# One block of a macaron encoder: attention scores from [qh; qh] and [ql; 0] times [kh; kl], k of both heads transposed in one group, changed orders in the feed-forward and at its joint, last output block in halves

## The chip, the cores and the metric

The kernel runs on one core of one Trainium2 chip. The metric is the device time of one execution in microseconds (us). Before the change it is 1906.35 us, the median of three runs (1906.08 to 1906.64).

## What is computed

The input x has 1024 rows (frames) of 1024 columns, float32. One layer is computed, in three steps:

```python
x = x + 0.5 * swiglu(rms_norm(x, n1), w1_in, w1_out)        # D = 1024, F = 2816
x = x + stick_breaking_attention(rms_norm(x, nm), w_qkv, q_gain, k_gain, w_o)
x = x + 0.5 * swiglu(rms_norm(x, n2), w2_in, w2_out)
# attention, 16 heads of 64: q, k are rms-normed per head and have a gain
z = (q @ k.T) / 8                                           # s < t only
A[t, s] = sigmoid(z[t, s]) * prod(1 - sigmoid(z[t, j]) for s < j < t)
o = A @ v                                                   # then o @ w_o
```

## The kernel before, in words

**Split products.** TensorE multiplies operands of type fp32r. Every float32 operand is therefore split in a high part and the rest ("h" and "l", `split` L195: a copy on ScalarE, then a subtraction on VectorE or GpSimd), and a product is three matmuls: h·h, h·l and l·h (`mm3` L301).

**Feed-forward** (`ffn_in` L430, `ffn_out` L558, used twice). The products are done by a scheme with seven products of half-size blocks instead of eight. `ffn_in` goes over 11 slices q of the hidden columns; for each one `prepare` (L466) splits the weights and their mixtures s1, s2, s3, s4 into units ("u" tiles), and `seven` (L494) runs seven products of 12 matmuls for the gate and seven for the up half. Two of the banks go on accumulating after a copy: `copy` (L497) takes the bank "ka" to SBUF on ScalarE, and the next product into "ka" can start after it. ScalarE thus does the units' high parts (L196), the copies (L499) and the silu of the gates (L547). `ffn_out` runs seven products m in the order of `SEVEN`, each on four banks, one for each block of 128 rows. The last, m = 6, ends block by block: block t takes the last three of the six chunks (five slices, 15 matmuls of 512 columns), then `result(t)` (L619) adds the bank to x, then `at(...)` is called, which in the second feed-forward stores the rows to the output (L1349). The results of the product before it, m = 2, are done late, during the first chunks of the last one.

**Joint between the first feed-forward and the attention** (`at` L872). After block t of the last product, rows that are normed already are transposed into the banks "mb" (`turn_rows`, L287) and split, and the next rows are squared (ScalarE), their rates taken (GpSimd) and scaled (`norm` L251, VectorE). The numbers (2, 0, 0, 1) at L900 say how many row blocks are transposed after block 0, 1, 2, 3.

**Attention** (L912 to L1247). The heads are done in eight pairs p. For each pair `qkv` (L956) makes q, k and v of the next pair in 24 pieces ("fills"), on banks "bq"; q and k are kept in a tile qk, whose columns are six groups of 64: q of both heads, then k of head 1 twice, k of head 0 twice, scaled by the norm's factor on GpSimd (L996, L999). `prep_q` (L1023) transposes the q of both heads of half the frames with four transposes of 128x128 (L1016), and puts, for each head, the high part on one half of the partitions of a tile q_s (ScalarE, L1020) and the rest on the other half (VectorE, L1021). `prep_k` (L1031) does the same for one head and half the frames: the transposed k stands on both halves of the partitions; kh_s holds its high part, kl_s the rest. A score step (`scores` L1038) is then two matmuls with the same stationary operand (L1057, L1058):

```python
for i in range(2):
    pe.matmul(z[:, : off + n], q, state["k", hd, kb][i][:, keys], start=i == 0, stop=i == 1)
```

[qh; ql]·[kh; kh] gives qh·kh + ql·kh, and [qh; ql]·[kl; kl] gives the terms with kl. Two sigmoids follow on ScalarE (L1062), the running product on VectorE (L1067) and the weights on GpSimd (L1074). The weights are transposed (L1098), split and multiplied by v (L1119, `values` L1080). Sums of a pair are written to DRAM in two parts (L1132) and loaded again before the output projection (L1143).

**What sets the order.** Each pair has four parts a, b, c, d of 10, 14, 21 and 16 units of planned time (`PARTS` L39). In part a the scores of head 1, second half of the frames are made; in b head 0, first half; in c head 1, first half; in d those of head 0, second half of the next pair. `put(part, t, f)` gives a step a planned time; the steps are emitted in that order (L1246), and a scheduler of the framework then orders each engine's instructions by this priority as their operands come ready; `issue_after` adds an edge between two instructions. The preparations stand at: q of the second half at c 15.0, k of head 0 of the second half at c 17.0, k of head 1 of the second half at d 8.0, q of the first half at a 5.0, k of head 0 of the first half at a 7.5, k of head 1 of the first half at b 10.7 (L1216 to L1222). All large transfers, the raw weights of pair p+2 among them (c 14.0, c 15.0, d 9.0, d 10.0, L941), are issued in order from SP's queue.

Of the kernel before, what the change touches and what calls it, by code (L numbers as in the profile page):

```python
# [52 lines left out]
)  # L53

# [59 lines left out]
def macaron_kernel(ctx, tc, x, g1, w1_in, w1_out, gm, w_qkv, gq, gk, w_o, g2, w2_in, w2_out, out):  # L114
# [155 lines left out]
    def turned(xs, tb, bk, tl=None):  # L270
# [13 lines left out]
        for d in range(2):  # L284
# [5 lines left out]
            split(tp, xh[dst], xl[dst])  # L290
# [139 lines left out]
    def ffn_in(pl, w_in, keep, tl, hb, right, last):  # L430
# [35 lines left out]
        def prepare(raw, behind=None):  # L466
# [20 lines left out]
            marks["s3"] = marks["unit"]  # L487
# [6 lines left out]
        def seven(us, result):  # L494


            def copy(b):  # L497
                s = small(pl, "s")
                act.activation(s, b, AF.Copy)  # L499
                return s  # L500
# [13 lines left out]
            s2 = copy(a)  # L514
            product(c, us["s4"], b22, False)
# [11 lines left out]
        for q in range(1, NQ):  # L527
# [21 lines left out]
            us = prepare(stream(pl, w_in, q, 1), before[1, 1][:, 0:1] if q == 1 else None)  # L549
# [8 lines left out]
    def ffn_out(pl, w_out, keep, x_from, ahead, at):  # L558
# [37 lines left out]
        for m, tag, fresh, goes in SEVEN:  # L596
# [11 lines left out]
            def add(ts, cs):  # L608
                for c in cs:
                    (wh, wl), (hh, hl), _ = ops[c]  # L610
                    for i, q in enumerate(CHUNKS[c]):
                        for t in ts:
                            s = slice(t * P, (t + 1) * P)
                            mm3(
                                bs[t], [((hh[:, i, s], hl[:, i, s]), (wh[:, i], wl[:, i]))],
                                fresh and q == 0, q == NQ - 1, not fresh,
                            )

            def result(t, bs=bs, goes=goes):  # L619
                for (th, h), sign in goes:  # L620
                    xc = x_sb[h][:, 4 * (1 - th) + t, :]
                    dve.scalar_tensor_tensor(out=xc, in0=bs[t], scalar=0.5 * sign, in1=xc, op0=ALU.mult, op1=ALU.add)
# [43 lines left out]
    with pools(*RAWS) as pr:  # L666
# [200 lines left out]
        with banks("ps2"), pools(*SECOND) as pl:  # L867
# [4 lines left out]
            def at(x_sb, m, where, ops):  # L872
# [25 lines left out]
                elif m == 6 and str(where).startswith("block"):  # L898
                    t = int(where[-1])
                    turn_rows("mb", (2, 0, 0, 1)[t])  # L900
                    squares(pn, row, (t,), half[:, t : t + 1], (1,))
                    last_norm = lambda: pending.extend(norm(pn, row, (t,), gain_m, half[:, t : t + 1], pooled=True))
                    if t < 3:
                        last_norm()
                    else:
                        late.append(last_norm)
# [9 lines left out]
    with ExitStack() as stack:  # L916
# [39 lines left out]
        def qkv(p, state):  # L956


            def start(half):
                if half:  # L960
                    state["v"] = pl[f"vst{p % 2}"].tile([P, NT, 4, DH], F32R, name="vst", bufs=1)
                state["qk", half] = pl[f"qk{half}"].tile([P, 4, 6, DH], F32, name=f"qk{half}", bufs=1)
# [14 lines left out]
            def finish(half, i, ps, room):  # L977
# [16 lines left out]
                rk = r[:, :, 0:1].unsqueeze(3).to_broadcast([P, 4, 2, DH])  # L994
                kv = qk[:, :, 2:3, :].to_broadcast([P, 4, 2, DH])
# [23 lines left out]
        def parts(tp, g, hi, lo):  # L1019
            act.activation(hi, tp, AF.Copy, scale=g)  # L1020
            dve.scalar_tensor_tensor(out=lo, in0=tp, scalar=g, in1=hi.bitcast(F32), op0=ALU.mult, op1=ALU.subtract)  # L1021

        def prep_q(state, half):  # L1023

            tp = turned_qk(state["qk", half], 0)
            for i in range(2):
                own, other = slice(i * DH, (i + 1) * DH), slice((1 - i) * DH, (2 - i) * DH)
                q_s = state["q", i, half] = pl[f"st{half}"].tile([P, NHALF], F32R, name=f"q_s{half}")
                parts(tp[own], g_sb[0][own], q_s[own], q_s[other])

        def prep_k(state, hd, half):  # L1031

            kh_s, kl_s = state["k", hd, half] = [
                pl[f"st{half}"].tile([P, NHALF], F32R, name=f"k{n}_s{half}") for n in "hl"
            ]
            parts(turned_qk(state["qk", half], 4 - 2 * hd), g_sb[1], kh_s, kl_s)

        def scores(state, hd, half):  # L1038
# [3 lines left out]
            def step(tb, kb):  # L1042
# [7 lines left out]
                q = state["q", hd, half][:, (tb % 4) * P : (tb % 4 + 1) * P]  # L1050
# [6 lines left out]
                for i in range(2):  # L1057
                    pe.matmul(z[:, : off + n], q, state["k", hd, kb][i][:, keys], start=i == 0, stop=i == 1)  # L1058
# [21 lines left out]
        def values(state, p, hd, half):  # L1080

            own, other = slice(hd * DH, (hd + 1) * DH), slice((1 - hd) * DH, (2 - hd) * DH)
# [23 lines left out]
            def apply(sbs):  # L1106
# [19 lines left out]
                if hd == 1 and (p < NP - 2 or p == NP - 2 and half):  # L1126
# [3 lines left out]
                    split(o, oh, ol)  # L1130
# [28 lines left out]
        last_x = ((pool_e, 0, lambda: xl[:, KD - 1, T - P : T - P + 1].bitcast(F32)),)  # L1159
# [27 lines left out]
        for p in range(-1, NP):  # L1187
# [21 lines left out]
            if nxt is not None:  # L1209
# [6 lines left out]
                put("c", 15.0, partial(prep_q, nxt, 1))  # L1216
                put("c", 17.0 if p >= 0 else 20.0, partial(prep_k, nxt, 0, 1))
                put("d", 8.0, partial(prep_k, nxt, 1, 1))
            if this is not None:
                put("a", 5.0, partial(prep_q, this, 0))  # L1220
                put("a", 7.5, partial(prep_k, this, 0, 0))
                put("b", 10.7, partial(prep_k, this, 1, 0))  # L1222
            if 0 <= p < NP - 2:

                held = (
                    ((pool_e, 1, lambda s=nxt: s["qk", 1][:, 0, 4, 0:1]),),
# [165 lines left out]
```

## Time and profile before

| | before |
|---|---|
| median of 3 runs | 1906.35 us (1906.08 to 1906.64) |
| the profiled execution | 1906.09 us |
| its span, first to last instruction | 1904.3 us |
| TensorE (PE) busy | 1892.7 us, 99% |
| VectorE (DVE), ScalarE (ACT), GpSimd (POOL) busy | 1230.2, 975.7, 1138.2 us |
| granted clock of TensorE | 1.000 |
| attention, from the first q to the end of the projection | about 660 to 1290 us of the span |

Times in the views are microseconds from the start of the span. A line is named L and its number in the listing; where a helper does the work, the line is the helper's. Matmuls are pipelined: the duration of one is longer than the distance to the next, so what a matmul costs is read from the starts of neighbours. PE stands for matmuls, PEld for the loads of stationary operands, SPq for the queue that issues transfers. "Idle" behind a row is the time that the engine stood still before it, and what ended it.

### The profile page before, as it was taken

How to read it: one execution, taken by the hardware profiler on the slowest of the kernel's cores; microseconds unless marked ns; L12 is line 12 of the kernel's file. 1: busy time of each engine (PE TensorE's matmuls, PEld its weight loads, DVE VectorE, ACT ScalarE, POOL GpSimd, SP SyncE). 2: the span in 40 equal slices, each digit the busy share in tenths (PEclk: the TensorE clock that was granted, in tenths of full speed). 3: DMA queues.
4: the chain of work that ended last, by engine and by line, in shares of the span. 5: the costliest groups of instructions: out<-in, count | busy, mean ns of one | idle time of the engine just before them, and what ended most of it. 6: DMA issues, size and time to landing. Idle time of an engine off the chain costs nothing.

```text
span 1904.3 us, 26681 instructions
## 1 busy us (share of the span) xinstructions
PE 1892.7 (99%) x9330; PEld 1620.3 (85%) x9330; DVE 1230.2 (65%) x1713; ACT 975.7 (51%) x1794; POOL 1138.2 (60%) x1063
## 2 busy tenths in 40 slices
PE   9999999999999999999999999999999999999999
PEld 8878888888888799999999997788888888888887
DVE  6856445635874758878888887567455445558645
ACT  7433433343434458888888886344333433343332
POOL 6766667655556746656665665215666666655554
PEclk9999999999999999999999999999999999999999
DMA  6233323337897411111111152612233323369973
GB/s 205 89 111 116 104 84 112 116 110 266 312 359 258 154 34 31 43 43 53 42 36 47 51 186 73 212 56 82 95 117 105 106 89 117 105 235 344 328 269 138
DMA packets 168983, 258.66 MB, mean 136 GB/s; under 512 B 11664, under 2 KB 82320, under 8 KB 168848
## 3 DMA queue, kind: packets, MB, share of 16 engines
q1 hardware_dynamic: 168704, 256.95, 39.5%
q8 instruction: 73, 1.20, 0.3%
q14 instruction: 62, 0.51, 0.1%
q10 hardware_dynamic: 144, 0.00, 0.0%
HBM read 197.14 MB, written 59.77 MB: 135 GB/s over the span
## 4 chain that ended last, share of the span: by engine, by line
PE 91%; DVE 6%; ACT 1%; issue 1%; POOL 1%; DMA 1%; SPq 0%; DVEq 0%; ACTq 0%; POOLq 0%
PE ka L308 6%; PE ka L309 6%; PE ka L310 6%; PE bq L308 5%; PE bq L310 5%; PE bq L309 5%; PE kc L309 4%; PE kc L308 4%; PE kc L310 4%; PE kb L309 4%; PE kb L310 4%; PE kb L308 4%; PE ma L308 4%; PE ma L310 4%; PE ma L309 4%; PE bz L1058 3%
## 5 line engine op out<-in xcount | busy, mean ns | idle before, releaser
L197 POOL TENSOR_TENSOR rp<-raw,rp 128x1024 fp32r<-128x1024 f32 x84 | 213.8, 2551 | 168.4 <-ACT rp L196 157.6
L197 POOL TENSOR_TENSOR u<-sf,u 128x512 fp32r<-128x512 f32 x160 | 227.8, 1425 | 136.1 <-ACT u L196 136.1
L197 POOL TENSOR_TENSOR u<-raw,u 128x512 fp32r<-128x512 f32 x128 | 187.3, 1466 | 142.1 <-ACT u L196 98.3
L196 ACT ACTIVATE u<-sf 128x512 fp32r<-128x512 f32 x160 | 100.8, 630 | 204.8 <-PE kb L309 87.1
L1074 POOL TENSOR_TENSOR w<-w,om 128x512 f32<-128x512 f32 (+4 forms) x128 | 140.8, 1104 | 97.2 <-DVE om L1067 83.8
L446 DVE TENSOR_TENSOR h<-h 128x512 f32<-128x512 f32 x110 | 135.4, 1234 | 85.9 <-POOL h L554 85.2
L308 PE MATMUL bq<-wqh,xh 128*128 128x384 f32 x512 | 174.5, 341 | 0.4
L310 PE MATMUL bq<-wqh,xl 128*128 128x384 f32 x512 | 172.0, 336 | 0.0
L196 ACT ACTIVATE rp<-rh 128x1024 fp32r<-128x1024 f32 (+1 forms) x78 | 76.4, 984 | 186.6 <-issue 61.2
L309 PE MATMUL bq<-wql,xh 128*128 128x384 f32 x512 | 171.9, 336 | 0.0
L576 DVE TENSOR_TENSOR raw<-raw 128x1024 f32<-128x1024 f32 (+1 forms) x60 | 94.3, 1574 | 107.6 <-DMA raw<-w_out 93.9
L196 ACT ACTIVATE u<-raw 128x512 fp32r<-128x512 f32 x128 | 80.2, 630 | 150.0 <-PE ka L309 100.7
L308 PE MATMUL ka<-xh,u 128*128 128x512 f32 x352 | 137.2, 390 | 1.9 <-ACT s L499 1.9
L308 PE MATMUL ma<-rp 128*128 128x512 f32 x352 | 137.0, 389 | 0.0
L310 PE MATMUL ka<-xh,u 128*128 128x512 f32 x352 | 137.0, 389 | 0.0
L310 PE MATMUL ma<-rp 128*128 128x512 f32 x352 | 136.9, 389 | 0.0
L309 PE MATMUL ka<-xl,u 128*128 128x512 f32 x352 | 136.9, 389 | 0.0
L309 PE MATMUL ma<-rp 128*128 128x512 f32 x352 | 136.9, 389 | 0.0
L554 POOL TENSOR_TENSOR h<-h,g 128x512 f32<-128x512 f32 x80 | 113.0, 1413 | 35.3 <-DVE h L503 33.5
L475 DVE TENSOR_TENSOR sf<-raw 128x512 f32<-128x512 f32 x80 | 80.2, 1003 | 78.0 <-POOL u L197 78.0
L1062 ACT ACTIVATE w<-bz,f 128x512 f32<-128x512 f32 (+1 forms) x192 | 113.7, 592 | 26.8 <-PE bz L1058 25.3
L197 DVE TENSOR_TENSOR rp<-rh,rp 128x1024 fp32r<-128x1024 f32 (+1 forms) x70 | 108.2, 1563 | 22.0 <-ACT rp L196 19.5
(309 smaller groups left out, 5457.8 us busy)
## 6 DMA issues: line engine op xcount, KB each, us to landing
raw<-w_out SPq DMA_DIRECT2D x120, 512.0 KB, 5.7
raw<-w_in SPq DMA_DIRECT2D x86, 512.0 KB, 3.6
k<-h SPq DMA_DIRECT2D x154, 256.0 KB, 2.0
rh<-k SPq DMA_DIRECT2D x64, 512.0 KB, 6.1
raw_qkv<-w_qkv SPq DMA_DIRECT2D x64, 192.0 KB, 3.0
x_keep<-x SPq DMA_DIRECT2D x32, 256.0 KB, 3.1
x<-x_keep SPq DMA_DIRECT2D x32, 256.0 KB, 5.4
raw<-w_out SPq DMA_DIRECT2D x24, 256.0 KB, 4.3
```

What stands on the lines that cost most here:

```text
L196: first = act.activation(hi, raw, AF.Copy).ins
L197: return first, (engine or dve).tensor_tensor(lo, raw, hi.bitcast(F32), op=ALU.subtract).ins
L308: pe.matmul(dst, ah, bh, start=start and i == 0, stop=False, skip_group_check=onto)
L309: pe.matmul(dst, ah, bl, start=False, stop=False, skip_group_check=onto)
L310: pe.matmul(dst, al, bh, start=False, stop=stop and i == n - 1, skip_group_check=onto)
L446: dve.tensor_tensor(src, hb[of[0]], hb[of[1]], op=getattr(ALU, of[2]))
L475: dve.tensor_tensor(f[n], x, y, op=op)
L554: pool_e.tensor_tensor(h, h, gs[k], op=ALU.mult)
L576: dve.tensor_tensor(w[0], w[0], w[1], op=getattr(ALU, W_OF[m][2]))
L1058: pe.matmul(z[:, : off + n], q, state["k", hd, kb][i][:, keys], start=i == 0, stop=i == 1)
L1062: marks["scored"] = act.activation(to, z, AF.Sigmoid, scale=state["f", half][:, sign, tb % 4, hd : hd + 1]).ins
L1074: marks["weighed"] = pool_e.tensor_tensor(wt[:, c1 : c0 + n], wt[:, c1 : c0 + n], om[:, c1 - 1 : c0 + n - 1], op=ALU.mult).ins
```

## The change

- **Scores.** A score step is still two matmuls, now with the stationary operands [qh; qh] and [ql; 0] and the same moving operand [kh; kl]. The copy of qh on the other half of the partitions is made by a DMA from SBUF to SBUF (two of 64x512 for each `prep_q`); the zeros of the ql tiles are written once. k stands once in qk; both heads are scaled by one GpSimd instruction and transposed by one group of four.
- **Places.** q of the second half moves to c 11.0, k of both heads of the second half stands at c 17.0; q of the first half moves to d 15.9 of the pair before; k of both heads of the first half stays at a 7.5. The first pair keeps c 15.0, c 20.0 and a 5.0.
- **Feed-forward.** In slice 2 the silu follows the copy of s2 and not the unit of s3; in slice 1 the unit s4 of the up half follows the gate's copy of s2.
- **Joint.** Rows are transposed after the blocks as (1, 1, 0, 1); the rates are taken apart from the norms; the norm of row 1 follows the result of block 2, the norm of row 2 the split of the transposed row 0; the first raw weights wait for a row block one earlier.
- **Last block.** In the second feed-forward block 3 is multiplied, added and stored in two halves of 256 columns.
- For the first half of the frames the split of a pair's sums has its subtraction on GpSimd.

```diff
+PREP = {"q1": ("c", 11.0), "k1": ("c", 17.0), "q0": ("d", 15.9), "k0": ("a", 7.5)}
...
-            split(tp, xh[dst], xl[dst])
+            marks["turned"] = split(tp, xh[dst], xl[dst])[1]
...
-                us["s4"] = unit(pl, f["s4"], pool_e)
+            with following(copied):
+                us["s4"] = unit(pl, f["s4"], pool_e)
...
             s2 = copy(a)
+            marks["s2"] = marks["copy"]
...
-                with following(marks["s3"] if q == 2 else None):
+                with following(marks["s2"] if q == 2 else None):
                     act.activation(g, g, AF.Silu)
...
             for t in range(4):
-                add([t], range(n, len(CHUNKS)))
-                if not late:
-                    result(t)
-                if last:
-                    at(x_sb, m, f"block {t}", ops)
+                for part in parts if last and t == 3 else (slice(0, NHALF),):
+                    add([t], range(n, len(CHUNKS)), part)
+                    if not late:
+                        result(t, n=part)
+                    if last:
+                        at(x_sb, m, f"block {t}", ops, part)
...
-                    turn_rows("mb", (2, 0, 0, 1)[t])
+                    turn_rows("mb", (1, 1, 0, 1)[t])
                     squares(pn, row, (t,), half[:, t : t + 1], (1,))
...
+                    if t == 0:
+                        pending.extend(norm(pn, row, (0,), gain_m, r=rate()))
+                    elif t < 3:
+                        late.append(rate())
+                        if t == 2:
+                            pending.extend(norm(pn, row, (1,), gain_m, r=late.pop(0), behind=marks["result"]))
                     else:
+                        pending.extend(norm(pn, row, (2,), gain_m, r=late.pop(), behind=marks["turned"]))
+                        late.append(lambda: pending.extend(norm(pn, row, (3,), gain_m, r=rate())))
...
-                pool_e.tensor_tensor(qk[:, :, 4:6, :], kv, rk, op=ALU.mult)
-                for to in (2, 3):
-                    rk = r[:, :, 1:2].to_broadcast([P, 4, DH])
-                    pool_e.tensor_tensor(qk[:, :, to, :], qk[:, :, 3, :], rk, op=ALU.mult)
+                rk = r[:, :, 0:2].unsqueeze(3).to_broadcast([P, 4, 2, DH])
+                pool_e.tensor_tensor(qk[:, :, 2:4, :], qk[:, :, 2:4, :], rk, op=ALU.mult)
...
+        def parts(pieces):
+            for tp, g, hi, _ in pieces:
+                act.activation(hi, tp, AF.Copy, scale=g)
+            for tp, g, hi, lo in pieces:
+                dve.scalar_tensor_tensor(out=lo, in0=tp, scalar=g, in1=hi.bitcast(F32), op0=ALU.mult, op1=ALU.subtract)
...
         def prep_q(state, half):
             tp = turned_qk(state["qk", half], 0)
+            pieces = []
+            for hd in range(2):
+                own, other = sides(hd)
+                if (hd, half) not in low_q:
+                    low_q[hd, half] = pl[f"st{half}"].tile([P, NHALF], F32R, name=f"ql{hd}_s{half}", bufs=1)
+                    pool_e.memset(low_q[hd, half][other].bitcast(F32), 0.0)
+                q_s = pl[f"st{half}"].tile([P, NHALF], F32R, name=f"qh{hd}_s{half}", bufs=1)
+                state["q", hd, half] = q_s, low_q[hd, half]
+                pieces.append((tp[own], g_sb[0][own], q_s[own], low_q[hd, half][own]))
+            parts(pieces)
+            for hd in range(2):
+                own, other = sides(hd)
+                q_s, _ = state["q", hd, half]
+                sp.dma_start(q_s[other].bitcast(F32), q_s[own].bitcast(F32))
+
+        def prep_k(state, p, half):
+            tp = turned_qk(state["qk", half], 2)
+            pieces = []
+            for hd in range(2):
+                own, other = sides(hd)
+                room = f"qk{1 - hd}" if half and p % 2 else f"st{half}"
+                k_s = state["k", hd, half] = pl[room].tile([P, NHALF], F32R, name=f"k{hd}_{room}", bufs=1)
+                pieces.append((tp[own], g_sb[1][own], k_s[own], k_s[other]))
+            parts(pieces)
...
-                q = state["q", hd, half][:, (tb % 4) * P : (tb % 4 + 1) * P]
+                q = [t[:, (tb % 4) * P : (tb % 4 + 1) * P] for t in state["q", hd, half]]
...
-                    pe.matmul(z[:, : off + n], q, state["k", hd, kb][i][:, keys], start=i == 0, stop=i == 1)
+                    pe.matmul(z[:, : off + n], q[i], state["k", hd, kb][:, keys], start=i == 0, stop=i == 1)
...
-                    split(o, oh, ol)
+                    split(o, oh, ol, dve if half else pool_e)
...
-        last_x = ((pool_e, 0, lambda: xl[:, KD - 1, T - P : T - P + 1].bitcast(F32)),)
+        last_x = ((pool_e, 0, lambda: xl[:, KD - 1, T - 2 * P : T - 2 * P + 1].bitcast(F32)),)
...
-        ffn_out(pl | pr, w2_out, keep, x_keep[1], ops, at)
+        ffn_out(pl | pr, w2_out, keep, x_keep[1], ops, at, [slice(n, n + NHALF // 2) for n in (0, NHALF // 2)])
```

## Rows read from the trace of the kernel before

**Rows 1.** The page's parts 1 and 2: TensorE's busy time with its count of matmuls, and the granted clock in 40 slices, in tenths of full speed (9 is 90% or more).
```profile
PE 1892.7 (99%) x9330; PEld 1620.3 (85%) x9330; DVE 1230.2 (65%) x1713; ACT 975.7 (51%) x1794; POOL 1138.2 (60%) x1063
...
PEclk9999999999999999999999999999999999999999
```

**Rows 2.** Who TensorE waited for in the whole span: total us, times, longest us.
```profile
PE ka L308 <- ACT s L499: 1.9, 2, 1.4
...
PE mb L287 <- DVE x L622: 1.5, 3, 0.5
PE bt L287 <- DVE xl L197: 0.5, 1, 0.5
```

**Rows 3.** Busy time by stretch, one stretch for one pair of heads (the first and the last of six equal ones): length, then busy us and instructions of PE, PEld, DVE, ACT, POOL, then granted clock, DMA share and GB/s.
```profile
711.40:774.06 62.66, 62.62 (x386) 58.99 (x386) 51.26 (x101) 50.91 (x112) 39.91 (x66) 1.00 0.14 43
...
1024.82:1087.53 62.71, 62.64 (x386) 58.99 (x386) 51.29 (x101) 50.92 (x112) 39.90 (x66) 1.00 0.15 47
```

**Rows 4.** The transposes of q and k: their group among the lines of PE (count, busy us, mean ns), and one group of four in the timeline of PE (start, length) with the matmuls behind it.
```profile
L1016 PE MATMUL bz<-ident,qk 128*128 128x128 f32 x192 | 28.9, 273 | 0.5 <-DVE w L1067 0.3
...
848.69 0.60 PE L1016 MATMUL bz<-ident,qk 128*128 128x128 f32 x4
849.04 0.36 PE L1058 MATMUL bz<-kh_s,q_s 128*128 128x256 f32 x1
849.25 0.28 PE L1058 MATMUL bz<-kl_s,q_s 128*128 128x256 f32 x1
849.36 0.34 PE L308 MATMUL bq<-wqh,xh 128*128 128x384 f32 x1
```

**Rows 5.** The second matmuls of the scores (L1058), by source line: the loads of their stationary operand, the matmuls (ns min/median/max), and what their engine's idle time before them waited for (us, times).
```profile
L1058 PEld LDWEIGHTS bz<-kl_s,q_s x192: 186/188/192, 694.3 to 1186.1; 128*128 128x128 f32 x192
L1058 PE MATMUL bz<-kl_s,q_s x192: 277/364/501, 694.4 to 1186.3; 128*128 128x512 f32 x96, 128*128 128x256 f32 x64, 128*128 128x384 f32 x32
...
  DVE kl_s L1021: 2.0, 8
```

**Rows 6.** ScalarE's scaled copies of q and k (64 and 128 partitions), and GpSimd's separate products for k of head 1, by source line: ns min/median/max.
```profile
L1020 ACT ACTIVATE q_s<-bz,gq_sb x32: 675/682/686, 686.9 to 1147.8; 64x512 fp32r<-64x512 f32 x32
L1020 ACT ACTIVATE kh_s<-bz,gk_sb x32: 679/690/847, 692.8 to 1159.3; 128x512 fp32r<-128x512 f32 x32
...
L999 POOL TENSOR_TENSOR qk<-qk,r x32: 622/626/1007, 687.3 to 1144.1; 128x256 f32<-128x256 f32 x32
```

**Rows 7.** The border of parts a and b in one pair: the first score of part b in the timeline of PE (its two matmuls), and the subtraction that makes kl_s for it in the timeline of DVE.
```profile
836.84 0.40 PE L1058 MATMUL bz<-kh_s,q_s 128*128 128x512 f32 x1
837.17 0.50 PE L1058 MATMUL bz<-kl_s,q_s 128*128 128x512 f32 x1
...
836.38 0.74 DVE L1021 SCALAR_TENSOR_TENSOR kl_s<-bz,gk_sb,kh_s 128x512 fp32r<-128x512 f32 x1
```

**Rows 8.** One pair on the transfer queue SP (the weights of a later pair, eight issues from the first to the last), and on PE the transposes at c 15.0 and the first score of part d.
```profile
869.44 18.82 SPq L941 DMA_DIRECT2D raw_qkv<-w_qkv  x8
...
866.87 0.60 PE L1016 MATMUL bz<-ident,qk 128*128 128x128 f32 x4
875.03 0.40 PE L1058 MATMUL bz<-kh_s,q_s 128*128 128x512 f32 x1
```

**Rows 9.** A store from SBUF that nothing else crowds, by issue: count, KB each, median us from issue to landing.
```profile
k<-h SPq DMA_DIRECT2D x154, 256.0 KB, 2.0
```

**Rows 10.** The last pair: stretch of 5 us (columns as in rows 3), eight loads of x on SP with their time to landing (min/median/max), and a score of part b on PE.
```profile
1140.00:1145.00 5.00, 4.91 (x30) 3.55 (x28) 4.65 (x15) 4.90 (x10) 3.33 (x8) 1.00 1.04 386
...
1141.87 4.52 SPq L1299 DMA_DIRECT2D x<-x_keep  x8
...
DMA to landing us min/median/max: 4.8/5.7/6.2
...
1149.76 0.39 PE L1058 MATMUL bz<-kh_s,q_s 128*128 128x512 f32 x1
```

**Rows 11.** The first feed-forward, slices 1 and 2: PE's longer wait for a copy (slice 2), and in ScalarE's timeline the rows ahead of the copies (in slice 1 two units, L196; in slice 2 a silu, L547), with the idle time before each.
```profile
116.03 0.50 PE L308 MATMUL ka<-xh,u 128*128 128x512 f32 x1 [1.42 <-ACT s L499]
...
74.53 1.15 ACT L196 ACTIVATE u<-sf 128x512 fp32r<-128x512 f32 x2 [2.27 <-DVE sf L475]
...
114.35 0.63 ACT L547 ACTIVATE g<-g 128x512 f32<-128x512 f32 x1 [4.73 <-DVE g L503]
```

**Rows 12.** The joint: eight late results on DVE, the last of three waits of the row transposes on PE, the scaling of row 2 on DVE and the wait of row 1's transposes.
```profile
644.79 4.86 DVE L622 SCALAR_TENSOR_TENSOR x<-mb,x 128x512 f32<-128x512 f32 x8
...
649.71 0.66 PE L287 MATMUL mb<-ident,xs 128*128 128x128 f32 x4 [0.54 <-DVE x L622]
...
664.03 1.42 DVE L263 SCALAR_TENSOR_TENSOR xs<-x,rs_y,gain 128x512 f32<-128x512 f32 x2 [1.44 <-POOL rs_y L220]
...
666.19 1.23 PE L287 MATMUL bt<-ident,xs 128*128 128x128 f32 x8 [0.53 <-DVE xl L197]
```

**Rows 13.** A run of 24 matmuls of 256 columns in the chain that ended last (start, length of the run), and the end of the kernel: a matmul of 512 columns in that chain, the last result on DVE and the last issue on SP.
```profile
27.84 2.88 PE kc L324 x24
...
1899.95 0.23 PE ma L308
...
1900.67 0.69 DVE L622 SCALAR_TENSOR_TENSOR x<-ma,x 128x512 f32<-128x512 f32 x1 [2.71 <-PE ma L310]
...
1901.39 0.33 SPq L1349 DMA_DIRECT2D out<-x  x1
```

More of the change, by code (lines that the diff above doesn't have):

```diff
@@ L464, in ffn_in, with prepare @@
         t3 = quarter(0, T1)
-        def prepare(raw, behind=None):
+        def prepare(raw, behind=None, copied=None):
             a11, a12, a21, a22 = (columns(raw[d], j) for j in range(2) for d in range(2))
@@ L556, in ffn_in, with ffn_out @@
         more.close()
-    def ffn_out(pl, w_out, keep, x_from, ahead, at):
+    def ffn_out(pl, w_out, keep, x_from, ahead, at, parts=(slice(0, NHALF),)):
         place["rp"] = 0
@@ L606, in ffn_out, with add @@
                     loaded.add((th, h))
-            def add(ts, cs):
+            ends = CHUNKS[-BY_BLOCK - 1][-1] if last and len(parts) > 1 else NQ - 1
+            def add(ts, cs, n=slice(0, NHALF)):
                 for c in cs:
@@ L614, in add, with result @@
                             mm3(
[L615 to L616 removed]
+                                bs[t][:, n], [((hh[:, i, s], hl[:, i, s]), (wh[:, i, n], wl[:, i, n]))],
+                                fresh and q == 0, q == NQ - 1 or (t == 3 and q == ends), not fresh or n != slice(0, NHALF),
                             )
[L619 removed]
+            def result(t, bs=bs, goes=goes, n=slice(0, NHALF)):
                 for (th, h), sign in goes:
[L621 to L622 removed]
+                    xc = x_sb[h][:, 4 * (1 - th) + t, n]
+                    marks["result"] = dve.scalar_tensor_tensor(
+                        out=xc, in0=bs[t][:, n], scalar=0.5 * sign, in1=xc, op0=ALU.mult, op1=ALU.add
+                    ).ins
             n = len(CHUNKS) - BY_BLOCK if last else len(CHUNKS)
@@ L870, in macaron_kernel, with at @@
             half = pn["xs"].tile([P, 4, 2], F32, name="half", bufs=1)
-            def at(x_sb, m, where, ops):
+            def at(x_sb, m, where, ops, part=None):
                 def row(tb, h):
@@ L961, in start @@
                     state["v"] = pl[f"vst{p % 2}"].tile([P, NT, 4, DH], F32R, name="vst", bufs=1)
-                state["qk", half] = pl[f"qk{half}"].tile([P, 4, 6, DH], F32, name=f"qk{half}", bufs=1)
+                state["qk", half] = pl[f"qk{half}"].tile([P, 4, 4, DH], F32, name=f"qk{half}", bufs=1)
                 state["ssq"] = pl["sq"].tile([P, 4, 4], F32, name="ssq", bufs=1)
@@ L1023, in prep_q, with sides @@
+        def sides(hd):
+            return slice(hd * DH, (hd + 1) * DH), slice((1 - hd) * DH, (2 - hd) * DH)
+        low_q = {}
         def prep_q(state, half):
             tp = turned_qk(state["qk", half], 0)
[L1026 to L1029, printed above, removed]
@@ L1080, in values @@
         def values(state, p, hd, half):
-            own, other = slice(hd * DH, (hd + 1) * DH), slice((1 - hd) * DH, (2 - hd) * DH)
+            own, other = sides(hd)
             tb0 = half * 4
@@ L1335, in macaron_kernel, with at @@
         lay_banks()
-        def at(x_sb, m, where, ops):
+        def at(x_sb, m, where, ops, part=slice(0, NHALF)):
             tbs, hs = (), ()
@@ L1348, in at @@
                 for h in hs:
-                    sp.dma_start(out[rows(tb), HALVES[h]], x_sb[h][:, tb, :])
-        ffn_out(pl | pr, w2_out, keep, x_keep[1], ops, at)
+                    sp.dma_start(out[rows(tb), HALVES[h]][:, part], x_sb[h][:, tb, part])
+        ffn_out(pl | pr, w2_out, keep, x_keep[1], ops, at, [slice(n, n + NHALF // 2) for n in (0, NHALF // 2)])
     after.close()
```

41 lines of the change are left out of this document (15 added, 26 removed).

## The prediction

> **What bounds the kernel now.** I read the busy times first: PE 1892.7 of 1904.3 us, at full granted clock in every slice [rows 1]. A busy PE need not be a full PE, so next came PE's waits: a few us in all, and the three that matter sit in the feed-forward and at the joint [rows 2]. Then the attention, cut into pairs of heads: every pair takes 62.7 us, PE is busy for 62.6 of them, VectorE for 51.3, ScalarE for 50.9, GpSimd for 39.9 [rows 3]. The matmuls stand close behind one another there (rows 4 are typical). So PE's instructions set the time nearly everywhere, and what the change is worth is (1) PE work that disappears, (2) PE waits that disappear, less (3) waits that appear.
>
> **The change, part by part.**
>
> *Transposes.* Before, a pair needs two groups of four for q and four for k; after, two and two. 16 groups of the 48 go, 64 transposes of 192. Mean duration is no price, since they overlap: four start at 848.69, the matmul behind starts at 849.04, and the next one is late as well (0.21 us after it where its twin needs 0.11) [rows 4]. So a group costs 0.35 + 0.10 = 0.45 us, 16 cost 7.2. Ends: 16 x 0.35 = 5.6, if the late neighbour is then paid by another transpose beside it; and 64 x 28.9/192 = 9.6 by busy time [rows 4]. I take 7.1, near the row of starts. Nothing covers this work: it is PE's own.
>
> *Score matmuls.* Two before, two after, with the same columns moved. What is new is that the two have different stationary operands. The trace has 192 loads for 192 second matmuls although the operand is the same one as in the first [rows 5]: the load is paid today. Price 0; above, see the rivals; a gain has no reason.
>
> *Copies and subtractions of k.* Four of 128x512 become four of 64x512 on ScalarE, and likewise on VectorE; half the partitions save nothing (0.68 against 0.69 us [rows 6]). GpSimd loses two products of 0.63 us for each half, 32 in all [rows 6]: it is idle a third of a pair [rows 3], so 0 on the path. The half of the sums' splits that moves to GpSimd, and the four clears of the ql tiles, fit in the same room: 0.
>
> *Border of a and b.* Today the preparations of q and of k for part b stand 2.5 planned units apart, and kl_s is done at 837.12, just when the second matmul of the first score wants it (0.33 us after the first, where 0.23 is usual) [rows 7]; the loads' idle time for kl_s is 2.0 us over 8 times [rows 5]. Moving q to d 15.9 takes two copies and two subtractions (0.68 each on ScalarE [rows 6]) out of that queue; k of head 1 comes in, but behind head 0. Against it, one tile now holds kh and kl, so the first matmul too must wait for the subtraction. Ends: all 2.0 us gone, or 0.5 us more in each of eight pairs (from 836.84 to 837.12, and the handover), +4.0. I take -0.7, nearer the first, as q's four instructions stood ahead of k's and k of head 1 stands behind.
>
> *q's copy by DMA.* Two transfers of 128 KB on SP for each `prep_q`, 32 in all. No row shows one from SBUF to SBUF; the nearest is a store of 256 KB, 2.0 us [rows 9]; in a crowded stretch a load lands after 5.7 [rows 10]. In a pair the q of the second half stands at c 11.0, ten units ahead of part d, about 10 us. SP has the raw weights to issue from 869.44, and the transposes at c 15.0 are at 866.87, so those of c 11.0 come near 863; the copies leave near 866, ahead of that batch, and land near 868 to 872, before d's first score at 875.03 [rows 8]. The q of the first half at d 15.9 again has ten units. Behind the waiting SP stand only raw weights for a pair later. So 0 in pairs 0 to 6. The last pair is tighter: DMA is full there (share 1.04), eight loads of x are issued from 1141.87 to 1146.4, and q is wanted at 1149.76 [rows 10]. Ahead of them the copy lands by about 1147; behind them at 1146.4 + 5.7 = 1152, 2 to 3 us late. I take +0.5, between 0 and +3.
>
> *Feed-forward edges.* PE waits twice for a copy, 1.9 us [rows 2]. In slice 1 ScalarE sits until 74.53 for the subtraction behind two units of the up half, and the copy of s2 stands behind them; in slice 2 it sits 4.73 us for a gate's sum before a silu, with the copy behind [rows 11]. The new edges put the copy ahead of both. A unit waiting for its own mixture may still stand before the second copy. I take -1.7; ends 0 and -2.2, the 1.9 and some 0.15 for each slow start behind a wait (the matmul at 116.03 takes 0.50 [rows 11]). The silus get later by less than a product; the up half reads them only 12 matmuls x 7 later.
>
> *Joint.* The two row blocks transposed after block 0 need banks that the eight late results clear at 1.2 us each until 649.65 [rows 12]: three waits, 1.5 us [rows 2]. With one row block after block 0 and the next after block 1, 15 matmuls of 0.23 us (3.4 us) later, two of the three go. Row 1's transposes wait 0.53 us for the split of row 0, which stands behind the scaling of row 2 [rows 12]; the new edge reverses them. I take -1.6 (0.54 + 0.54 + 0.53); ends 0 and -2.2 (all of 1.5 + 0.5, and slow starts). The norm of row 1, now behind block 2's result, still ends well before its transposes. Next late would be the rates on GpSimd, behind raw weights.
>
> *Last block in halves.* 15 matmuls of 0.23 become 30 of 0.12 (2.88/24 [rows 13]): +0.2. The last sum is half of 0.69: between 0.35 and 0.69, I take 0.43, -0.26. The last transfer, issued at 1901.39 with the span ending at 1904.3 [rows 13], is half as large: 0 to -0.7, I take -0.3. Together -0.4, ends +0.2 and -0.8.
>
> Sum: -7.1 - 0.7 + 0.5 - 1.7 - 1.6 - 0.4 = -11.0 us. The profiled execution took 1906.09 us, of which 1904.3 is span; the median is 1906.35, so the same sum from it gives **1895.3 us**. About 0.2%, 3.8 us, is what a measurement of this kernel can tell from no change.
>
> **The rivals.**
>
> *Only the transposes pay.* The scheduler places the freed copies and rows so that new waits replace those at the joint and in the feed-forward. For it: those waits are ordering effects, and every order moves. Against it: the edges name exactly the instructions in front. Time: 1906.35 - 7.2 = 1899.2.
>
> *The pair does not shorten.* If the chain score, sigmoid, running product, weight, transpose sets a pair and not PE, the freed time turns into waits. For it: VectorE and ScalarE are 82% busy [rows 3]. Against: 0.06 us idle on PE in 62.66. Then only 1.7 + 1.6 + 0.4 remain: 1902.7.
>
> *The copy of q is late in every pair (slower).* Place: SP, between c 11.0 and part d. If the scheduler lets the raw weights go first, the copies wait inside a batch that lasts 18.8 us. In the middle of it they leave at 878.8 and land at 880.8, where d's first score stands at 875.03 [rows 8]: 5.8 us for each of seven pairs, +40.6, 1936. It decides from 2.1 us for each pair on, which makes +15. Against it: the planned place is ahead of the batch by 3 units, and SP waits for nothing long there.
>
> *Two stationary operands cost a second load (slower).* If today's second matmul used the operand already loaded, 192 loads of 0.188 us would be new: up to +36, 1931. The rows speak against it: 192 loads for 192 such matmuls [rows 5]. The Trainium skill, page "TensorE: Matmul & The Clock Gate", section "Step-by-step: what each phase is for", says that loading and multiplying are separate so that one load can serve many matmuls; by that rule this change would give up a saving. Here the trace shows that this kernel does not use it.
>
> **How the numbers follow.** My forecast (between about 1892 and 1898) gets 0.69; only the transposes 0.14; no shorter pair 0.08; late in every pair 0.04; second load 0.01; the last 0.04 is a late copy in the last pair together with a missed term, near 1899. The low end adds the good bounds of edges, joint, border and tail (0.5 + 0.6 + 1.3 + 0.4) and the last pair's 0.5 and some of the transposes': 1891.5. The high end takes in only the transposes, with their lower bound, 1906.35 - 5.6: 1900.7. Faster by over 0.2% are the forecast, the transposes alone and the late last copy, with some of the third rival's: 0.90; within: 0.05; slower: 0.05.
>
> **What would show it.** The profile after should have 128 transposes of qk, pairs of about 61.7 us with PE still 99% busy, no wait for s L499, one short wait for "mb" left, the copies landing within 2 to 4 us. It is wrong if PE waits for q's copy or for k in front of parts b or d, if a pair stays near 62.7, or if PE's idle time at the joint only moves.

## The result, and the profile after the change

The changed kernel takes 1894.99 us (median of 6 runs, 1894.52 to 1895.31) against 1905.93 us of the kernel before (6 runs, 1905.59 to 1906.64): 10.9 us less, ratio 0.9941 (95% interval 0.9931 to 0.9952). Predicted were 1895.3 us. The profiled execution took 1895.31 us, its span is 1893.3 us. Line numbers below are those of the changed kernel, which lie 2 to 34 behind those of before.

First the page's busy times and TensorE's waits (total us, times, longest), which answer to [rows 1] and [rows 2].

```profile
PE 1885.7 (100%) x9281; PEld 1616.6 (85%) x9281; DVE 1229.9 (65%) x1708; ACT 976.9 (52%) x1794; POOL 1122.3 (59%) x1041
...
PEclk9999999999999999999999999999999999999999
...
PE ma L310 <- DVE x L629: 0.5, 1, 0.5
PE bt L1131 <- DMA x<-x_keep: 0.4, 1, 0.4
PE bo L1152 <- ACT th L198: 0.3, 1, 0.3
PE mb L289 <- DVE x L629: 0.2, 1, 0.2
```

The waits for the copy s (1.9 us) and for xl (0.5) are gone, and "mb" is down from 1.5 to 0.2. The largest new one is "ma" for a sum x, 0.5 us; it sits in the last block. The two of 0.4 and 0.3 us behind it in the list are new too and sit in the last pair of heads. Next the pairs of heads (columns as in [rows 3]) and the transposes of q and k (as the first row of [rows 4]).

```profile
706.50:768.40 61.90, 61.85 (x378) 58.14 (x377) 50.70 (x100) 51.24 (x113) 38.42 (x64) 1.00 0.17 50
1013.57:1075.50 61.93, 61.90 (x378) 58.22 (x377) 50.74 (x100) 51.22 (x114) 38.38 (x64) 1.00 0.18 56
```
```profile
L1028 PE MATMUL bz<-ident,qk 128*128 128x128 f32 x128 | 19.3, 273 | 0.1
```

A pair has 8 matmuls less on PE (378 for 386) and ends sooner by some 0.8 us; from the first score of b in one pair to that of the next it is 61.85 where it was 62.70. PE still fills it: 0.05 us idle. GpSimd lost 1.5 us of work in each pair, but it was and is idle a third of the time; that this moved nothing is shown below, by the run with the transposes put back.

The places where single steps were forecast follow. The copy of q by DMA, by source line (issues on SP with ns min/median/max, then its landing):

```profile
L1058 SPq DMA_DIRECT2D qh_s<-qh_s x32: 461/468/544, 683.2 to 1130.8; - x32
...
DMA to landing us min/median/max: 2.2/2.2/4.3
```

No PE wait names it. In the last pair its two issues leave at 1129.73, ahead of the loads of x from 1131.47, so the half microsecond set aside for that pair was not needed. The border of parts a and b in one pair, in the timelines of ScalarE, VectorE and PE (start, length; [rows 7]), and last who waited for VectorE's subtractions of that source line in the whole span (us, times; [rows 5] has 2.0 us over 8 times for kl_s):

```profile
766.80 1.38 ACT L1033 ACTIVATE k_st<-bz,gk_sb 64x512 fp32r<-64x512 f32 x2 [0.34 <-PE bz L1028]
...
768.22 1.53 DVE L1035 SCALAR_TENSOR_TENSOR k_st<-bz,gk_sb,k_st 64x512 fp32r<-64x512 f32 x2 [1.27 <-ACT k_st L1033]
...
769.01 0.50 PE L1091 MATMUL bz<-k_st,qh_s 128*128 128x512 f32 x1
769.35 0.40 PE L1091 MATMUL bz<-k_st,ql_s 128*128 128x512 f32 x1
...
  PEld bz L1091: 1.8, 8
```

VectorE starts its first subtraction only behind both copies of ScalarE. The first score of b starts 0.05 us after the first subtraction of the two ends (768.96), and slowly: 0.34 us to the next where 0.23 is usual. Before, the second matmul came 0.33 us behind the first as well [rows 7], but the first was on time; now the first comes 0.28 us behind a matmul of 384 columns, where 0.17 is usual. So the border got 0.1 us worse in a pair, and of the 2.0 us of the loads' idle time 1.8 are left. The feed-forward's two edges in ScalarE's timeline ([rows 11]) and the row transposes of the joint on PE ([rows 12]):

```profile
74.05 0.58 ACT L501 ACTIVATE s<-ka 128x512 f32<-128x512 f32 x1
75.06 0.64 ACT L198 ACTIVATE u<-sf 128x512 fp32r<-128x512 f32 x1 [0.43 <-DVE sf L477]
...
112.12 0.58 ACT L501 ACTIVATE s<-ka 128x512 f32<-128x512 f32 x1
115.86 0.63 ACT L550 ACTIVATE g<-g 128x512 f32<-128x512 f32 x1 [3.15 <-DVE g L505]
```
```profile
645.31 0.66 PE L289 MATMUL mb<-ident,xs 128*128 128x128 f32 x4 [0.24 <-DVE x L629]
649.22 1.03 PE L289 MATMUL mb<-ident,xs 128*128 128x128 f32 x8
...
661.98 1.03 PE L289 MATMUL bt<-ident,xs 128*128 128x128 f32 x8
```

The copies of slices 1 and 2 now stand ahead of the unit and of the silu. At the joint one short wait is left. Last, the end of the kernel on PE and VectorE ([rows 13]):

```profile
1887.28 0.28 PE L312 MATMUL ma<-rp 128*128 128x256 f32 x1
1888.07 0.39 PE L310 MATMUL ma<-rp 128*128 128x256 f32 x1 [0.52 <-DVE x L629]
1888.29 0.28 PE L311 MATMUL ma<-rp 128*128 128x256 f32 x1
...
1887.59 0.42 DVE L629 SCALAR_TENSOR_TENSOR x<-ma,x 128x256 f32<-128x256 f32 x1 [1.10 <-PE ma L312]
1890.16 0.42 DVE L629 SCALAR_TENSOR_TENSOR x<-ma,x 128x256 f32<-128x256 f32 x1 [2.15 <-PE ma L312]
```

The second half's first matmul starts 0.79 us after the last one of the first half, where 0.12 is usual: it stands until VectorE has read the first half (1887.59 + 0.42 = 1888.01) out of the same bank. The stores of the halves land after 1.7 us.

Where the time came from, as differences of the same PE landmarks in the two traces: the start +0.59 (another profile of the same code), slices 1 and 2 of the first feed-forward -2.45, joint -1.66, attention to the start of the second feed-forward -7.93, the last block with its store +0.44. Together -11.0, the difference of the spans.

### The profile page after: what moved, and what is told of

It is laid out like the page before. It is cut to its first block, busy times and chain, and to the rows that moved or that the text cites. A ratio compares the mean times of both kernels' runs of the same rounds, so it can differ in the third digit from the quotient of the medians.

```text
span 1893.3 us, 26643 instructions
## 1 busy us (share of the span) xinstructions
PE 1885.7 (100%) x9281; PEld 1616.6 (85%) x9281; DVE 1229.9 (65%) x1708; ACT 976.9 (52%) x1794; POOL 1122.3 (59%) x1041
## 4 chain that ended last, share of the span: by engine, by line
PE 97%; DVE 1%; ACT 1%; DMA 0%; POOL 0%; issue 0%; SPq 0%; DVEq 0%; POOLq 0%
PE ka L311 6%; PE ka L310 6%; PE ka L312 6%; PE bq L312 5%; PE bq L311 5%; PE bq L310 5%; PE kc L311 4%; PE kc L310 4%; PE kc L312 4%; PE ma L310 4%; PE ma L312 4%; PE ma L311 4%; PE kb L311 4%; PE kb L310 4%; PE kb L312 4%; PE bo L1152 4%
## 5 line engine op out<-in xcount | busy, mean ns | idle before, releaser
L199 POOL TENSOR_TENSOR rp<-raw,rp 128x1024 fp32r<-128x1024 f32 x84 | 209.5, 2499 | 173.3 <-ACT rp L198 162.3
L310 PE MATMUL ma<-rp 128*128 128x512 f32 (+1 forms) x357 | 138.1, 387 | 0.5 <-DVE x L629 0.5
L312 PE MATMUL ma<-rp 128*128 128x512 f32 (+1 forms) x357 | 137.8, 386 | 0.0
L311 PE MATMUL ma<-rp 128*128 128x512 f32 (+1 forms) x357 | 137.8, 386 | 0.0
```

The source lines that it names most:

```text
L199: return first, (engine or dve).tensor_tensor(lo, raw, hi.bitcast(F32), op=ALU.subtract).ins
L310: pe.matmul(dst, ah, bh, start=start and i == 0, stop=False, skip_group_check=onto)
L311: pe.matmul(dst, ah, bl, start=False, stop=False, skip_group_check=onto)
L312: pe.matmul(dst, al, bh, start=False, stop=stop and i == n - 1, skip_group_check=onto)
```

## The experiments

All were timed against the kernel before on the same chip. The medians of before differed by chip (1905.93 with the changed kernel, then 1906.02, 1905.96 and 1905.53), so kernels timed on different chips are compared by their distance to it: the changed kernel stands at -10.9.

**One part alone, from the kernel before.** Each applies the hunks of the diff that belong to one part.

*Attention alone.*

> The kernel before with the attention part of the change alone (scores, k of both heads turned at once, q's copy by DMA, new places). My theory, that PE's work sets the pair and 16 groups of four transposes less are worth 0.44 us each, with the border of a and b unchanged: -7 to -8 us (1898.4 from 1905.9). By the prediction's terms -7.1 - 0.7 + 0.5 = -7.3. Rival, the pair is set by a chain of ScalarE and VectorE: within 1 us of before. Rival, late copies of q or second loads: slower by 15 us or more.

Measured: 1899.14 us (1899.09 to 1899.41), -6.9, ratio 0.9964 (0.9952 to 0.9977). The prediction's -7.3 holds, the theory's -7 to -8 is missed by 0.1; both rivals are out. From the first score to the start of the second feed-forward PE's starts move by -7.8, nearly as in the full change; 0.8 us of it are lost again between the first q and the first score. The split of the sums that moved to GpSimd is in this part and was not tried by itself.

*Edges in feed-forward alone:* `with following(copied)` for s4, and the silu behind `marks["s2"]`.

> The kernel before with the two edges in feed-forward alone. The trace of after puts slices 1 and 2 of the first feed-forward at -2.4 us and the second feed-forward at 0: 1903.5. The prediction's term was -1.7 (1904.2). Rival, the freed copies only move the waits: 0 (1905.9).

Measured: 1903.64 us, -2.4, ratio 0.9988 (0.9979 to 0.9997). PE's starts move by -0.76 in slice 1 and -1.74 in slice 2, and by no more than 0.3 anywhere else; the wait for s is gone from the waits. The freed copies move no wait.

*Joint alone:* `turn_rows("mb", (1, 1, 0, 1)[t])` with its norms and marks.

> The kernel before with the joint alone (one row block after block 0 and one after block 1, edges for the norms of rows 1 and 2). Prediction -1.6 (1904.3), the trace of after says -1.7 for this stretch. Rival, idle time at the joint only moves: 0 (1905.9).

Measured: 1903.52 us, -2.5, ratio 0.9987 (0.9978 to 0.9995). The waits for "mb" and "xl" are gone. By PE's landmarks -2.1 lies before the first q, and -0.9 between it and the first score; with attention alone that second stretch was 0.8 longer, and in the full change it is unchanged (-0.06). Why the stretch moves this way was not tried.

*Last block in halves alone:* the loop over `part`.

> The kernel before with the last block in halves alone. The trace of after says +0.5 (1906.4): the second half's first matmul waits 0.5 us for VectorE to read the first half out of the same bank, more than the shorter last sum and store give back. By the prediction's term -0.4 (1905.5). Both lie near the resolution of the times, so the profile's last matmul and last store decide.

Measured: 1906.41 us, +0.4, ratio 1.0002 (0.9993 to 1.0011): the times alone can't tell it from nothing. The profile can: it has the same new wait, "ma" for x, 0.5 us.

The four parts alone add up to -6.9 - 2.4 - 2.5 + 0.4 = -11.4, against -10.9 for all together.

**One part undone, from the changed kernel.** The last block whole again: `ffn_out(...)` without its list of two slices.

> The changed kernel with the last block undone: block 3 is multiplied, added and stored as a whole again. By the trace of after and the part tried alone (+0.4): 0.4 to 0.5 us faster than the changed kernel, 1894.5, and no wait of PE for the sum of the last block. By the prediction's term 0.4 slower, 1895.4.

Measured: 1894.24 us (1893.79 to 1894.65), -11.7 to before, ratio 0.9939 (0.9926 to 0.9951): 0.8 us better than the changed kernel by the medians, 0.4 by the traces of the last block. The halves, as they stand, cost time.

Twice the transposes of k:

```diff
-            for i in range(4):
+            for i in [*range(4), *range(4)] if a0 else range(4):
```

> The changed kernel with each group of four transposes of k issued twice into the same bank, so that PE does as many transposes as before. If PE's own work is what the transposes were worth: 16 groups of 0.44 us come back, +7.0 (1902.0); bounds +5.6 and +9.6 as in the prediction. Rival, the pair is set by ScalarE's and VectorE's chain and the gain came from fewer copies and products: within 1 us of the changed kernel (1895).

Measured: 1901.34 us, -4.6, so +6.3 against the changed kernel, 0.40 us for each of 16 groups; between the first b scores of neighbouring pairs +0.83. One such pair, with the columns of [rows 3]:

```profile
770.04:832.73 62.69, 62.66 (x386) 59.03 (x385) 50.75 (x100) 51.35 (x113) 38.31 (x63) 1.00 0.17 51
```

The copies, products and waits stay those of the changed kernel, GpSimd's 38.3 us too, and the pair takes what it took before (62.70). So PE's own work sets the pair, and in a steady pair the transposes are all that paid. Over all pairs they are not: from the first score to the last the changed kernel is 7.8 us shorter than before, and with the transposes put back it loses 6.1 of them. The other 1.7 lie before the first b score (0.4) and behind that of the seventh pair, p = 6 (1.3); what pays there was not tried.

q at its places of before:

```diff
-PREP = {"q1": ("c", 11.0), "k1": ("c", 17.0), "q0": ("d", 15.9), "k0": ("a", 7.5)}
+PREP = {"q1": ("c", 15.0), "k1": ("c", 17.0), "q0": ("a", 5.0), "k0": ("a", 7.5)}
```

> The changed kernel with q prepared at its places of before (c 15.0 and a 5.0), the copy by DMA kept. Theory: the copy is free only because it has ten planned units ahead of its part. From c 15.0 it has some 8 us and stands on the queue beside the batch of raw weights; issued inside the batch it lands near 879 in the pair of rows 8, where part d wants it at 875: up to +4 to +5 us in each of seven pairs; from a 5.0 it has some 5 us, of which ScalarE and the copy take about 4.5. Forecast +4 to +35, with PE waiting for a DMA at the scores. Rival, the copy is hidden wherever it stands: within 0.5 us of the changed kernel (1895), and no such wait.

Measured: 1901.85 us, -4.1, so +6.8. The size lies in the forecast, its reason doesn't. Copies land late in places (2.2/2.5/6.6 us), but no idle time of PE names one. Its waits, and then the border of a and b in the timelines of ScalarE, VectorE and PE of this kernel:

```profile
PE bz L1091 <- DVE k_st L1035: 2.5, 6, 0.4
...
PE bo L1152 <- DVE tl L199: 1.1, 7, 0.2
```
```profile
890.23 1.39 ACT L1033 ACTIVATE qh_s<-bz,gq_sb 64x512 fp32r<-64x512 f32 x2
893.06 1.39 ACT L1033 ACTIVATE k_st<-bz,gk_sb 64x512 fp32r<-64x512 f32 x2
...
891.65 1.51 DVE L1035 SCALAR_TENSOR_TENSOR ql_s<-bz,gq_sb,qh_s 64x512 fp32r<-64x512 f32 x2 [0.50 <-ACT qh_s L1033]
894.48 1.53 DVE L1035 SCALAR_TENSOR_TENSOR k_st<-bz,gk_sb,k_st 64x512 fp32r<-64x512 f32 x2
...
895.28 0.50 PE L1091 MATMUL bz<-k_st,qh_s 128*128 128x512 f32 x1 [0.41 <-DVE k_st L1035]
```

q's two copies and two subtractions stand ahead of k's on both engines, and the first score of b waits 0.41 us for the first subtraction of k. It starts 0.75 us behind the matmul before it, where the changed kernel has 0.28: 0.47 of the 1.0 us by which a steady pair got longer. Another 0.4 is the second wait above, for a low part of the weights (tl): its subtraction stands on VectorE behind the two of q of the second half (863.88 to 865.39 us), and PE's next start comes 0.63 us behind the one before, where 0.23 is usual. What the move of q bought is thus room on ScalarE and VectorE, ahead of k and of the weights. Time for the DMA can count in the last pair alone: there the copies leave behind the loads of x and land at 1148.86, and the first score of b stands at 1149.19, 65.05 us behind that of the pair before (61.03 in the changed kernel). PE did later work meanwhile, so that from the seventh pair on only 1.0 us is lost.

One stationary operand for both matmuls of a score: `q[i]` becomes `q[0]`, so the product with ql is left out and that with qh is added twice.

> The changed kernel with the same stationary operand, [qh; qh], in both matmuls of a score (the term of ql is left out). Theory: the second load was paid before and is paid with either operand: 384 loads in the trace, time within 0.3 us of the changed kernel (1895.0). Rival, two different operands cost a second load: 192 x 0.188 = up to 36 us faster (1859).

Measured: 1895.13 us, -10.8, so +0.1; the trace has 384 loads as with two operands:

```profile
L1091 PEld LDWEIGHTS bz<-k_st,qh_s x256: 186/188/192, 690.2 to 1168.6; 128*128 128x128 f32 x128
...
L1091 PEld LDWEIGHTS bz<-k_qk,qh_s x128: 186/188/192, 743.9 to 1174.4; 128*128 128x128 f32 x128
```

The rival of a second load is out.

**Copy and subtraction in turn.** This undoes the order in `parts`; that of before was copy, subtraction, copy, subtraction for q.

```diff
-            for tp, g, hi, _ in pieces:
-                act.activation(hi, tp, AF.Copy, scale=g)
             for tp, g, hi, lo in pieces:
+                act.activation(hi, tp, AF.Copy, scale=g)
                 dve.scalar_tensor_tensor(out=lo, ...)
```

> The changed kernel with copy and subtraction of the first head emitted before copy and subtraction of the second, so that VectorE need not wait for both copies. Theory: at the border of a and b the first score waits for the first subtraction, which starts only behind both copies; 0.69 us earlier, the wait and the slow start behind it (0.2 us for each of seven pairs) go: -1.0 to -1.6 (1893.7). Rival, the subtractions then stand apart in VectorE's queue and delay running products: 0 to +2 (1895 to 1897).

Measured: 1899.09 us, -6.4, so +4.1 by the medians and +4.5 by the distance to before: my theory fell; the rival had the sign, and its +2 was too little. The border itself did get what it should, as PE's rows show (0.24 us to the second matmul, no wait); but ScalarE's second copy now waits for VectorE's first subtraction, 24 times in the 32 preparations (lines from there on are one lower in this kernel):

```profile
891.24 0.69 ACT L1033 ACTIVATE k_st<-bz,gk_sb 64x512 fp32r<-64x512 f32 x1 [0.34 <-PE bz L1028]
891.82 0.48 ACT L198 ACTIVATE th<-bt 128x384 fp32r<-128x384 f32 x1
892.74 0.68 ACT L1033 ACTIVATE k_st<-bz,gk_sb 64x512 fp32r<-64x512 f32 x1 [0.44 <-DVE k_st L1034]
...
893.16 0.40 PE L1090 MATMUL bz<-k_st,qh_s 128*128 128x512 f32 x1
893.40 0.40 PE L1090 MATMUL bz<-k_st,ql_s 128*128 128x512 f32 x1
```

Summed by source line, ScalarE's idle time before these copies, as far as it waited for VectorE (us, times), and PE's waits:

```profile
  DVE k_st L1034: 7.2, 12
  DVE ql_s L1034: 3.3, 8
  DVE k_qk L1034: 2.8, 4
```
```profile
PE bo L1151 <- DVE tl L199: 1.5, 7, 0.2
PE bt L1130 <- POOL w L1104: 1.1, 1, 1.1
```

13.3 us of ScalarE's time go into waiting for the other reader of the same bank (in the changed kernel ScalarE waits for PE alone before these copies), and the parts of the weights (tl) and the last pair's weights come late: +0.35 in a steady pair, +2.2 from the first b score of pair 6 to the end of the scores. The Trainium skill, page "PSUM — Partial Sum Buffer", section "PSUM bank collisions raise a hardware error", says that two engines are kept from one bank in the same group of 32 partitions, reads included, while different groups may be read at once. The waits agree in that reads too are kept apart (0.44 us in the row at 892.74); but the two heads stand on different partitions, so by the rule these waits would not be needed. That the shared bank is their reason is an argument: beside the gain, which both only read, it is all that the two instructions have in common. Two heads on two banks were not tried.

**A bank of its own for the second half.** The last 15 matmuls of the second half go to a bank "mb", and its first 18 are added to x ahead.

```diff
+                spare = bank("mb")
+                result(3, n=parts[1])
...
-                                bs[t][:, n], [...],
+                                (spare if own else bs[t])[:, n], [...],
-                                fresh and q == 0, ...
+                                fresh and q == 0 or own and q == ends + 1, ...
```

> The changed kernel with the last 15 matmuls of the second half of block 3 on a bank of its own; the sum of its first 18 is added to x ahead, one more instruction on VectorE. Theory, the loss of the halves is the wait for VectorE's reading of the same bank: the wait of 0.5 us and its slow start go, last matmul 0.7 us earlier, time -0.6 to -0.9 (1894.3), and the halves then give the -0.4 of the prediction against a whole block. Rival, the second half starts late for another reason (30 short matmuls, loads of operands): no change (1895.0).

Measured: 1894.28 us (1893.62 to 1894.55), -11.3, ratio 0.9939 (0.9927 to 0.9952); by the medians 0.7 better than the changed kernel, by the distance to before 0.3, by PE's landmarks 0.76 in the last block. The last matmul of the first half and the first of the second in PE's timeline:

```profile
1886.62 0.28 PE L312 MATMUL ma<-rp 128*128 128x256 f32 x1
1886.74 0.28 PE L310 MATMUL mb<-rp 128*128 128x256 f32 x1
```

0.12 us apart instead of 0.79, with the same 30 short matmuls. The shared bank was the cause.

**Combinations.**

> The changed kernel with both edits, a bank of its own for the second half and copies and subtractions in turn. If the two gains add: -1.6 to -2.5 (1893.0), faster than before by 13 us and than the changed kernel.

> The changed kernel with the last block whole again and copies and subtractions in turn: -0.6 and -1.0 to -1.6, 1893.2; 0.3 us above the version with the other bank if that one works as the theory says, equal or below if it does not.

Measured: 1898.07 and 1899.06 us, -7.5 and -6.5: both missed, by the loss of the copies in turn. They compare the two ends of the kernel on one chip: the bank of its own is 1.0 us better than the whole block by the medians, whose ranges overlap, and 0.4 by the spans of the profiled executions (1896.3 and 1896.7).

The best versions are thus the whole block (1894.24) and the bank of its own (1894.28), both 0.6% faster than before; by the distance to before (-11.7 and -11.3) the whole block leads, against the spans above. Their medians lie under the fastest run of the changed kernel (1894.52), but the ranges overlap: the better of the three can't be told from the times alone.

## Why the prediction was right, and where it was not

The bound was read rightly: PE's work sets the pair, so what leaves PE leaves the time. All four rivals are out: the edges and the joint pay alone, the pairs got shorter, no idle time of PE names q's copy, and one operand has as many loads as two. By its own steps, predicted and measured:

| step | predicted | measured |
|---|---|---|
| transposes | -7.1 | -6.3 (put back) |
| score matmuls, two operands | 0 | +0.1 with one |
| border of a and b | -0.7 | no saving, 0.1 worse in a pair |
| q's copy | 0, last pair +0.5 | no wait, 0 |
| attention together | -7.3 | -6.9 alone, -7.9 in the trace |
| edges in feed-forward | -1.7 | -2.4 alone, -2.5 in the trace |
| joint | -1.6 | -1.7 in the trace, -2.5 alone |
| last block in halves | -0.4 | +0.4 alone, +0.4 in the trace |
| sum | -11.0 | -10.9 |

*Transposes.* 0.45 us for a group, from starts, was near: 0.40 measured by putting them back, 0.85 for the two groups of a pair in the trace. The bound by busy time (9.6) was the wrong end: a group's 0.60 us of busy time runs on into the matmul behind it, which starts after 0.35 [rows 4].

*Border.* This step failed. The saving did not come: by the rows of the border, what q's move freed was taken back by the one tile for kh and kl, whose first score waits for a subtraction that stands behind both heads' copies. The prediction had k of head 1 "behind head 0"; its copy stands ahead of head 0's subtraction. And the sum held the step for small, while 6.8 us hang on the places and 4.1 to 4.5 on the order of copies and subtractions, which the prediction costed at nothing. "Copies and subtractions of k: 0" was true of their durations and silent on their order.

*Edges.* The mechanism was right and the term too small: I held back part of the 1.9 us of waits for a unit that might stand before the second copy; it didn't, and some 0.3 us for each slow start behind a wait came on top (2.5 in PE's starts against 1.9 of waits). Its end of -2.2 was too near as well.

*Joint.* Two of the three waits for "mb" and the one for xl went as said, and the trace has the step's size. Alone the joint gave -2.5, more than its end of -2.2: by the landmarks 0.9 us lie behind the first q, in a stretch that the prediction didn't look at, and why is open.

*Last block.* This step failed in its sign. It counted the durations of both halves and forgot that they share a bank, which VectorE must read between them. PE's last matmul starts 1.1 us later than with a whole block (0.67 for the delayed start, 0.1 for the slow start behind it, 0.3 for the 30 starts of 0.12 in place of 15 of 0.23), and from there to the end of the span 0.6 us less pass (3.41 for 4.03). With a bank of its own the last matmul comes only 0.30 us later than with a whole block, so that the halves are 0.3 us shorter by these landmarks: near the term predicted, though the times can't tell it. The Trainium skill, page "PSUM — Partial Sum Buffer", section "PSUM bank collisions raise a hardware error", states the rule that spoke against this part, for disjoint columns of one bank too, and the prediction didn't weigh it; the row of the wait (0.52 us) agrees with it.

With the parts alone the errors are +0.4 (attention), -0.7 (edges), -0.9 (joint) and +0.8 (last block): they nearly cancel, and so do those of the trace (-0.6, -0.8, -0.1, +0.8, and +0.6 at the start). That the sum came within 0.1 us is luck; the mechanism and the order of the terms are not.

## What to carry to other kernels

Where PE fills a stage without idle time, count the starts of what leaves PE, and the rest of the change is a matter of keeping its operands early enough; then ask of each preparation in which order two engines read its bank, since that order was worth 4 us here and the durations nothing. Cutting the last block in two lost 0.4 us while the halves shared a bank, and by the traces gained 0.3 without. A saving shown by undoing a part alone (6.8 for the places, 6.3 for the transposes, 4 for the order) is not a share of the whole: they add up to more than the 6.9 us that the parts brought together.

## What the runs showed of the hardware

A copy of 128 KB from SBUF to SBUF by DMA landed after 2.2 us, where a store of 256 KB took 2.0 ([rows 9]) and the last two stores, of 128 KB, 1.7. Loads of stationary operands are the same 384 whether two matmuls in a row share the operand or not, and the time is the same to 0.1 us. Matmuls of 256 columns stand 0.12 us apart, those of 512 0.23. In the rows shown a matmul that follows a wait of PE, or of its load, needs 0.1 us more before the next one starts, so a wait costs more than its own length: the 0.52 us in the last block delayed PE by 0.67 and its neighbour by 0.10 more.
